# Two of the four parts of a causal convolution, first half: diagonal matmuls on TensorE in place of VectorE and ScalarE/GpSimd

## The chip, the cores and the metric

One NeuronCore of a Trainium2 chip runs the whole kernel. The metric is the device time of one execution in microseconds (us); lower is better. The kernel before has a median of 1479.4 us over three runs (1476.76 to 1481.39).

## What is computed

One layer of a sequence model on 1024 tokens of width 1024. What matters here, cut from the reference:

```python
p = h @ w_in                                   # 1024 -> 2*512 (conv) + RWKV inputs
u, u_gate = jnp.split(p_conv, 2, axis=-1)
u = u * jax.nn.sigmoid(u_gate)                 # 512 channels
u = causal_dwconv(u, conv_dw_w, conv_dw_b)     # 31 taps per channel, padded by 30 at the front
u = jax.nn.silu((layer_norm(u, LN_EPS) * conv_ln_g + conv_ln_b))
...                                            # RWKV branch: a recurrence over tokens gives y
m = jnp.concatenate([u, y], axis=-1) @ w_out   # token mix
x = x + gt_m * rms_norm(m, mix_post_g)
...                                            # feed-forward: w_up, 3-tap conv, silu gate, w_down
```

The depthwise convolution has 512 channels, so four parts of 128 channels (one channel per partition), and 31 taps. Everything is float32.

## The kernel before, in words

**Tiling.** Activations are kept transposed, channels on partitions and tokens on the free axis. The 1024 tokens are done in two halves of 512; the RWKV recurrence goes in four quarters of 256 tokens (`unit` prepares a quarter, with `prep`, `inverse` and `merge`; `chain` runs the recurrence over it; `finish` normalises it). Projections use float32 split in two float32r numbers: `weight` (L135 to L142) loads a 256 KB slab with SyncE (L138), rounds it on ScalarE (L140) and subtracts on GpSimd (L142). `project` then issues three matmuls per block of 128 inputs, high by high, high by low, low by high (L158 to L160). A projected tile of 128 outputs is two slabs, so 24 matmuls of 128x512. It goes into a PSUM bank of tag "m", of which there are two. Slabs have three buffers.

**The stage around the change.** After the first half's projections are done, the program writes, in this order: `filler[0] = conv(0, accs, 8)`; `lora` and `group_out`, the second half's projections for the RWKV branch (13 tiles, each drained by `shifted`); unit 2; `gate_in` and `glu`, the second half's other projections (10 tiles, and the gate's own matmuls at L491 to L494). `shifted` (L346) and `glu` (L364) end with `next(filler[0], None)`, so each finished tile lets the convolution issue a further piece. Unit 1 and the chains of quarters 0 and 1 stand before this in the program under a raised priority, and run at the same time. After it come `conv_norm` (layer norm and silu of the convolution), `split_in` into the high and low operands, then `out_proj_q` and `channel_in_q` for quarters 0 and 1, and the up-projection `up` of the feed-forward, which fills TensorE for most of the rest.

**Who orders the work.** A planner in the compiler places each instruction on its engine by priority and by its own estimate of when operands are ready; the order on an engine is then fixed. `tc.keep_in_program_order(i)` pins single taps to their place on the engine; in `conv` these are the first tap of every eight and ScalarE's operations.

**The convolution** is `conv` (L375). `load` (L380 to L387) makes the padded input of one part, 30 + 512 columns, in a slot of tag "cu" (one buffer, parts 0 to 2) or "cu3" (part 3): GpSimd clears 30 columns (L382), SyncE loads the rest (L385). `vector` does parts 0, 1 and 2 on VectorE, 31 operations each: the first at L393, then a multiply-add per tap at L396, accumulated in a PSUM bank of tag "v", the last one written to `cacc0` to `cacc2`. `scalar` does part 3: ScalarE multiplies by a tap (L400 for the first, L403 after it, into two slots of tag "ctmp") and GpSimd adds (L404). `taps` is 8: each call of the filler issues eight steps. The second half's convolution is the same generator with `taps` 3, called from `up`.

**What waits for it.** `conv_norm` (L420 to L443) needs all four parts. The operands that `split_in` writes (`hh_o`, `hl_o`, L453 and L454) lie in the slots that held the second half's normalised input, so they wait for the last of `glu`'s matmuls on them too. `out_proj_q(0)` (tile `o`) needs these and the first quarter from `finish`; `out_proj_q(1)` needs the second quarter, which `mix_in_q` loads (tile `q_mi`, L824) after `finish(1)`, and that follows the chain of quarter 1.

**Other names that the change touches.** The tiles `v` of the RWKV branch (tag "v" of pool `rw`, five buffers) are allocated in `v_tiles` (first half) and `group_back` (second half, loaded at L541). The slots of tag "ctmp" have 512 columns and also serve `ada_rest`, `conv_norm` and the tiles `m` of the out projection.

Of the kernel before, what the change touches and what calls it, by code (L numbers as in the profile page):

```python
# [7 lines left out]
F32 = mybir.dt.float32  # L8
F32R = mybir.dt.float32r
AF = mybir.ActivationFunctionType  # L10
ALU = mybir.AluOpType
# [3 lines left out]
P = 128  # L15
D = 1024
T = 1024
HT = 512
NK = D // P
QT = HT // 2  # L20
# [5 lines left out]
KC = 31  # L26
# [41 lines left out]
def build(nc, tc, I, O):  # L68
    V, S, G, TE = nc.vector, nc.scalar, nc.gpsimd, nc.tensor
# [7 lines left out]
    def slot(pool, tag, name, n=HT, bufs=1, dt=F32):  # L77
        return pool.tile([P, n], dt, name=f"{tag}_{name}", tag=tag, bufs=bufs)
# [14 lines left out]
    def col(name, j=0, n=1):  # L93
        o = _cols[name] + j
        return pv[:, o:o + n]
# [24 lines left out]
    th = mod[:, 0:8]  # L120
# [11 lines left out]
    def bank(name, tag="s", bufs={"m": 2, "s": 1, "w": 2, "c": 1, "y": 1, "v": 1}):  # L132
        return ps_pool.tile([P, 512], F32, name=name, tag=tag, bufs=bufs[tag])
# [11 lines left out]
    spare, rate = iter(()), 1  # L145
# [180 lines left out]
    cv = tc.alloc_tile_pool(name="cv", bufs=1, side="right")  # L326
    rw = tc.alloc_tile_pool(name="rw", bufs=1, reuse_waits="tile")
# [47 lines left out]
    def conv(half, accs, taps):  # L375

        cw = lambda ct, k: col("conv_w", ct * KC + k)

        def load(ct):
            u = slot(cv, "cu3" if ct == 3 else "cu", f"{half}_{ct}", 30 + HT)  # L380
            if half == 0:
                G.memset(u[:, 0:30], 0.0)  # L382
            else:
                nc.sync.dma_start(u[:, 0:30], ud[0][ct][:, HT - 30:])
            nc.sync.dma_start(u[:, 30:], ud[half][ct])  # L385
            accs[ct] = slot(cv, f"cacc{ct}", f"{half}_{ct}")
            return u  # L387

        def vector():

            for ct in range(3):
                u, acc = load(ct), bank(f"cv{half}_{ct}", "v")
                yield V.tensor_scalar(acc, u[:, 0:HT], cw(ct, 0), col("conv_b", ct), ALU.mult, ALU.add)  # L393
                for k in range(1, KC):
                    o = accs[ct] if k == KC - 1 else acc
                    yield V.scalar_tensor_tensor(o, u[:, k:k + HT], cw(ct, k), acc, ALU.mult, ALU.add)  # L396

        def scalar():
            u, acc = load(3), accs[3]
            yield S.activation(acc, u[:, 0:HT], AF.Identity, scale=cw(3, 0), bias=col("conv_b", 3))  # L400
            for k in range(1, KC):
                t = slot(cv, "ctmp", f"{half}_{k}", bufs=2)
                i = S.activation(t, u[:, k:k + HT], AF.Identity, scale=cw(3, k), bias=ZERO)  # L403
                G.tensor_tensor(acc, acc, t, ALU.add)  # L404
                yield i

        v, s = vector(), scalar()
        n = 0
        while n < 3 * KC:
            for j in range(taps):  # L410
                i = next(v, None)
                if i is not None and j == 0:
                    tc.keep_in_program_order(i)
                if n % 3 == 0:
                    i = next(s, None)
                    if i is not None:
                        tc.keep_in_program_order(i)
                n += 1
            yield

    def conv_norm(accs, half, b):
        s = slot(cv, "cu", f"s{half}", 30 + HT)[:, :HT]
        V.tensor_tensor(s, accs[0], accs[1], ALU.add)
        V.tensor_tensor(s, s, accs[2], ALU.add)
        V.tensor_tensor(s, s, accs[3], ALU.add)
        mean = bank(f"cm{half}", b)
        TE.matmul(mean, nmean, s, start=True, stop=True)
        s2 = slot(cv, "cu3", f"s2{half}", 30 + HT)[:, :HT]
        for ct in range(4):
            V.tensor_tensor(accs[ct], accs[ct], mean, ALU.add)  # L430
            sq = s2 if ct == 0 else slot(cv, "ctmp", f"sq{half}_{ct}", bufs=2)
            S.activation(sq, accs[ct], AF.Square, bias=ZERO)
            if ct:
                G.tensor_tensor(s2, s2, sq, ALU.add)
        rb = bcast(rstd(s2, f"cv{half}", ones, 1, 1.0 / CW, EPS_LN, tag="c", b=b), f"cv{half}", 1, b=b)
        for ct in range(4):
            V.tensor_tensor(accs[ct], accs[ct], rb, ALU.mult)
            t = slot(cv, "ctmp", f"th{half}_{ct}", bufs=2)
            S.activation(t, accs[ct], AF.Tanh, scale=col("ln_g", ct), bias=col("ln_b", ct))
            S.activation(accs[ct], accs[ct], AF.Identity, scale=col("ln_g", ct), bias=col("ln_b", ct))  # L440
            V.scalar_tensor_tensor(accs[ct], t, 1.0, accs[ct], ALU.add, ALU.mult)
            if half:
                nc.sync.dma_start(mixed[half][ct], accs[ct])  # L443
# [7 lines left out]
    def split_in(x, hh, hl):  # L451

        S.copy(hh, x)  # L453
        V.tensor_tensor(hl, x, hh.bitcast(F32), ALU.subtract)  # L454
        return hh, hl
# [50 lines left out]

    def v_tiles(half):

        new = lambda q, g: rw.tile([P, 2, QT], F32, name=f"v{2 * half + q}{g}", tag="v", bufs=5)
        t = {(q, g): new(q, g) for q, g in ((0, 0), (0, 1), (1, 0), (1, 1))}  # L510
        return [[t[q, g] for q in range(2)] for g in range(2)]

# [24 lines left out]
    def group_back(q, g):  # L537
        kvr = []
        for x in range(3):
            t = rw.tile([P, 2, QT], F32, name=f"{'kvr'[x]}{q}{g}", tag="kvr"[x], bufs=(3, 5, 3)[x])  # L540
            nc.sync.dma_start(t, kvd[g][x][:, q % 2])  # L541
            kvr.append({q % 2: t})
        return kvr
# [274 lines left out]
    mtags = ("ctmp", "ctmp", "cu", "cu3", "cacc0", "cacc1", "cacc2", "cacc3")  # L818
# [205 lines left out]
    def unit(q, kvrs, la, before=None):  # L1024
# [4 lines left out]
        if before:  # L1029
            with first():  # L1030
# [6 lines left out]
    kvrs = [in_group(h, 0, 0, vt[0])]  # L1037

    ctags = ("ctmp", "cu", "ctmp", "cu3", "cacc0")
    spare = ada_rest(range(3), lambda i, n: slot(cv, ctags[i % 5], n, 30 + HT if ctags[i % 5][:2] == "cu" else HT,  # L1040
                                                 2 if ctags[i % 5] == "ctmp" else 1)[:, :HT],
                     4, lambda n: slot(cv, "cacc2", n), "v")
    kvrs.append(in_group(h, 0, 1, vt[1]))
# [26 lines left out]
    accs = [None] * 4  # L1070
# [18 lines left out]
    with first():  # L1089
        for k in range(4):  # L1090
            split_in(accs[k], *h[k])
    ms = [slot(cv, t, f"m{m}", 30 + HT if t[:2] == "cu" else HT, 2 if t == "ctmp" else 1)[:, :HT] for m, t in enumerate(mtags)]
    with tc.high_priority(offset=500000):
        mix_in_q(0, h)
        sums = out_proj_q(0, h, ms)
# [11 lines left out]
    accs = [None] * 4  # L1107
# [29 lines left out]
def layout(inp):  # L1137

    a = {k: np.asarray(v) for k, v in inp.items()}
    c = np.ascontiguousarray  # L1140
    vec = lambda v: v.reshape(-1, P).T
    mu = a["rwkv_mu"][0]
    mu = np.concatenate([vec(mu[:1664 + 128]), np.pad(np.tile(mu[1792:], 3), (0, 32)).reshape(P, 1)], 1)
    taps = lambda w: w.reshape(w.shape[0], -1, P).transpose(2, 1, 0).reshape(P, -1)
    pv = np.concatenate([
        vec(a["c"][0]), vec(a["ada_b"][0]), vec(a["mix_pre_g"][0]), vec(a["mix_post_g"][0]),
        vec(a["ffn_pre_g"][0]), vec(a["ffn_post_g"][0]), taps(a["conv_dw_w"][0]),
        vec(a["conv_dw_b"][0]), vec(a["conv_ln_g"][0]), vec(a["conv_ln_b"][0]), mu,
        vec(a["w0"][0]), vec(a["a0"][0]), vec(a["k_k"][0]), vec(a["k_a"][0]),
        vec(a["r_k"][0].reshape(-1)), vec(a["lnx_g"][0]), vec(a["lnx_b"][0]),  # L1150
        taps(a["ffn_dw_w"][0]), vec(a["ffn_dw_b"][0])], 1)

    mt = lambda w: w.reshape(w.shape[0] // P, P, -1, P).transpose(2, 1, 0, 3).reshape(-1, P, w.shape[0])
    w_in = a["w_in"][0]
    cols = []
    for t in range(4):
        cols += [t, 4 + t]
    cols += [20, 21]
    for p in range(4):
        cols += [12 + p, 16 + p, 8 + p]  # L1160
    win = mt(w_in[:, :22 * P])[cols]
    winl = w_in[:, 22 * P:].reshape(8, P, 1, 32).transpose(1, 0, 2, 3).repeat(3, 2).reshape(P, 768)
    ada = a["ada_w"][0]
    am = ada.reshape(8, P, 6, 2, HT).transpose(2, 3, 0, 1, 4)
    ada1, ada2 = am[:2], am[2:]
    return {
        "pv": c(pv), "cst": constants(),
        "w2a2": c(np.concatenate([a["w2"][0], a["a2"][0]], 0)),
        "g2a": c(a["g2"][0][:128]), "g2b": np.tile(a["g2"][0][128:], (3, 1)),
        "xT": c(a["x"][0].T.reshape(8, P, 2, HT).transpose(2, 0, 1, 3)),  # L1170
        "xR": c(a["x"][0][HT:].reshape(4, P, 2, HT)), "ada1": c(ada1), "ada2": c(ada2), "w_in": c(win), "w_inl": c(winl),
        "w_out": c(mt(a["w_out"][0])), "w_up": c(mt(a["w_up"][0])),
        "w_down": c(mt(a["w_down"][0])),
    }
# [15 lines left out]
```

## Time and profile before

| what | value |
|---|---|
| median of three runs | 1479.4 us |
| the profiled execution's own time | 1478.22 us |
| its span in the trace | 1476.4 us |
| mean granted TensorE clock | 0.964 |
| TensorE matmul / weight load busy | 93% / 76% |
| VectorE, ScalarE, GpSimd busy | 62%, 46%, 53% |

Busy time is the union of an engine's instructions as the trace has them. A matmul of 128x512 lasts 0.39 us in the trace but the next one starts 0.23 us later, because matmuls overlap; a row of TensorE's busy time therefore says when it had something in flight, and the weight loads (PEld), which do not overlap each other, say better how much more would fit. The span is cut into stretches below: 206 to 467 us is the stretch of the second half's projections, 467 to 584 us that of the out projection of the first half, and from 584 us on TensorE runs the feed-forward.

### The profile page before, as it was taken

What the parts mean: (1) busy time and instruction counts of PE and PEld (TensorE: products, weight loads), DVE (VectorE), ACT (ScalarE), POOL (GpSimd) and SP (SyncE); (2) the same over time, 40 slices, a digit from 0 to 9 for tenths busy, and PEclk for the clock granted to TensorE, in tenths of its full rate; (3) what the DMA queues carried; (4) which work ended last, traced back from release to release, by engine and by line L of the source; (5) the groups of instructions that cost most, each with busy time, mean ns of one, the idle gap of its engine ahead of it and who ended that gap; (6) DMA issues with size and microseconds to landing.
All of it is one profiled execution on the core that took longest, in us unless ns stands there. A gap on an engine that the chain in (4) does not pass through costs nothing.

```text
span 1476.4 us, 23402 instructions
## 1 busy us (share of the span) xinstructions
PE 1379.4 (93%) x8412; PEld 1115.5 (76%) x8412; DVE 915.0 (62%) x1427; ACT 682.0 (46%) x1234; POOL 783.0 (53%) x716
## 2 busy tenths in 40 slices
PE   3999989999899997999999999999998999999995
PEld 2787867777577885777788787777887888888884
DVE  7667669899765466888779965562027555551102
ACT  5445354365553465444555454644233444443221
POOL 2545654588653354555666654457446555454443
PEclk9999989999899896999999999999999999999997
DMA  9394572345323753235337345883335323233332
GB/s 358 118 351 139 171 202 93 116 121 152 97 79 106 184 161 106 66 90 150 96 107 217 122 147 188 295 285 91 94 96 183 110 94 99 95 98 93 92 98 75
DMA packets 168484, 208.02 MB, mean 141 GB/s; under 512 B 64112, under 2 KB 79088, under 8 KB 168368
## 3 DMA queue, kind: packets, MB, share of 16 engines
q1 hardware_dynamic: 167792, 205.48, 44.5%
q8 instruction: 66, 1.08, 0.3%
q10 hardware_dynamic: 576, 1.05, 0.2%
q14 instruction: 50, 0.41, 0.1%
HBM read 172.39 MB, written 34.08 MB: 140 GB/s over the span
## 4 chain that ended last, share of the span: by engine, by line
PE 67%; DVE 18%; DMA 6%; issue 3%; ACT 2%; SPq 2%; POOL 1%; DVEq 0%; POOLq 0%; ACTq 0%
PE up L158 9%; PE up L159 9%; PE up L160 9%; PE d L160 5%; PE d L158 5%; PE d L159 5%; DVE cv L396 2%; PE o L160 1%; PE o L158 1%; PE o L159 1%; DVE rkp L599 1%; DVE bk L601 1%; DVE t_dx L678 1%; PE s L621 1%; PE hn L708 1%
## 5 line engine op out<-in xcount | busy, mean ns | idle before, releaser
L142 POOL TENSOR_TENSOR wl_up<-w_up,wh_up 128x512 fp32r<-128x512 f32 x176 | 236.6, 1346 | 190.3 <-ACT wh_up L140 173.3
L140 ACT CAST wh_up<-w_up 128x512 fp32r<-128x512 f32 x176 | 108.9, 619 | 198.2 <-PE up L159 121.3
L142 POOL TENSOR_TENSOR wl_dn<-w_dn,wh_dn 128x512 fp32r<-128x512 f32 x96 | 116.8, 1220 | 118.6 <-ACT wh_dn L140 117.0
L158 PE MATMUL up<-hh_o,wh_up 128*128 128x512 f32 x352 | 141.3, 402 | 4.3 <-DVE q_za L949 4.2
L158 PE MATMUL up<-hh_f,wh_up 128*128 128x512 f32 x352 | 138.0, 392 | 4.1 <-DVE q_za L949 4.1
L160 PE MATMUL up<-hh_o,wl_up 128*128 128x512 f32 x352 | 141.7, 403 | 0.0
L159 PE MATMUL up<-hl_o,wh_up 128*128 128x512 f32 x352 | 140.7, 400 | 0.0
L160 PE MATMUL d<-ah,wl_dn 128*128 128x512 f32 x352 | 139.4, 397 | 1.0 <-POOL wl_dn L142 1.0
L159 PE MATMUL d<-al,wh_dn 128*128 128x512 f32 x352 | 139.4, 396 | 0.0
L158 PE MATMUL d<-ah,wh_dn 128*128 128x512 f32 x352 | 139.3, 396 | 0.0
L160 PE MATMUL up<-hh_f,wl_up 128*128 128x512 f32 x352 | 137.5, 391 | 0.0
L159 PE MATMUL up<-hl_f,wh_up 128*128 128x512 f32 x352 | 137.4, 390 | 0.0
L396 DVE SCALAR_TENSOR_TENSOR cv<-cu,pv,cv 128x512 f32<-128x512 f32 x174 | 130.2, 748 | 2.3
L994 DVE TENSOR_SCALAR mo_f<-d,mod 128x512 f32<-128x512 f32 x16 | 12.0, 749 | 180.9 <-ACT q_sqd L993 169.6
L140 ACT CAST wh_dn<-w_dn 128x512 fp32r<-128x512 f32 x96 | 56.0, 584 | 146.6 <-PE d L159 121.5
L944 DVE SCALAR_TENSOR_TENSOR q_za<-up,pv,q_za 128x510 f32<-128x510 f32 x88 | 65.6, 745 | 88.4 <-ACT q_za L942 88.2
L404 POOL TENSOR_TENSOR cacc<-cacc,ctmp 128x512 f32<-128x512 f32 x60 | 79.0, 1316 | 48.8 <-ACT ctmp L403 38.5
L158 PEld LDWEIGHTS up<-hh_o,wh_up 128*128 128x128 f32 x352 | 67.4, 192 | 19.3 <-DVE q_za L949 4.8
L158 PEld LDWEIGHTS up<-hh_f,wh_up 128*128 128x128 f32 x352 | 66.5, 189 | 18.6 <-ACT wh_up L140 4.5
L160 PEld LDWEIGHTS d<-ah,wl_dn 128*128 128x128 f32 x352 | 66.1, 188 | 17.6 <-POOL wl_dn L142 1.9
L160 PEld LDWEIGHTS up<-hh_o,wl_up 128*128 128x128 f32 x352 | 67.4, 191 | 14.9 <-issue 0.5
L158 PEld LDWEIGHTS d<-ah,wh_dn 128*128 128x128 f32 x352 | 66.1, 188 | 16.2 <-ACT wh_dn L140 0.4
(449 smaller groups left out, 3466.8 us busy)
## 6 DMA issues: line engine op xcount, KB each, us to landing
w_up<-w_up SPq DMA_DIRECT2D x176, 256.0 KB, 2.6
w_dn<-w_down SPq DMA_DIRECT2D x80, 256.0 KB, 2.7
w_o<-w_out SPq DMA_DIRECT2D x48, 256.0 KB, 3.4
aw_ada<-ada SPq DMA_DIRECT2D x32, 256.0 KB, 5.4
act<-q_za SPq DMA_DIRECT2D x22, 256.0 KB, 2.1
ax<-act SPq DMA_DIRECT2D x22, 256.0 KB, 4.6
ctmp_adb<-ada SPq DMA_DIRECT2D x20, 256.0 KB, 4.9
cu_adb<-ada SPq DMA_DIRECT2D x19, 256.0 KB, 4.5
```

What stands on the lines that cost most here:

```text
L140: S.copy(hi, w)
L142: e.tensor_tensor(lo, w, hi.bitcast(F32), ALU.subtract)
L158: TE.matmul(ps, wh[:, o], xh, start=k == 0, stop=False)
L159: TE.matmul(ps, wh[:, o], xl, start=False, stop=False)
L160: TE.matmul(ps, wl[:, o], xh, start=False, stop=k == K - 1)
L396: yield V.scalar_tensor_tensor(o, u[:, k:k + HT], cw(ct, k), acc, ALU.mult, ALU.add)
L404: G.tensor_tensor(acc, acc, t, ALU.add)
L599: V.tensor_tensor(pic(rkp[x][:, :, 1 + hh, :])[r], part(kkn, x)[r], half(eprev, x)[r], ALU.mult)
L601: V.tensor_tensor(bk[r, :, 1 - hh, :], v3(k)[r], v3(einv)[r], ALU.mult)
L621: TE.matmul(pss[hh][:, d], bk[r, ci(x, d)], rkp[x][r, d, 0:2 + hh:1 + hh, :], start=True, stop=True)
L678: V.tensor_tensor(t[:, i], u.unsqueeze(2).broadcast_to([P, n, n, n]), v.rearrange("p s c -> p c s").unsqueeze(1).broadcast_to([P, n, n, n] ...
L944: V.scalar_tensor_tensor(a[:, 2:], ps[:, 0:HT - 2], fw(0), a[:, 2:], ALU.mult, ALU.add)
```

## The change

Parts 0 and 1 of the first half stay on VectorE. Parts 2 and 3 become matmuls: for each tap a diagonal 128x128 matrix with the tap's weights (made on the host, a new input `cdiag` of 4 x 128 x 3968 float32) times the shifted input. As in the projections, weights and input are split into high and low, three matmuls per tap. Part 3 is issued whole at the fourth call of the filler, part 2 whole at the ninth. The second half's convolution is not changed.

```diff
+        def tensor(cts):
+            for ct in cts:
+                u, ps = load(ct), bank(f"cd{half}_{ct}", "m")
+                uh = slot(cv, "ctmp", f"uh{half}_{ct}", 30 + HT, 2, F32R)
+                ul = slot(cv, "ctmp", f"ul{half}_{ct}", 30 + HT, 2, F32R)
+                S.copy(uh, u)
+                G.tensor_tensor(ul, u, uh.bitcast(F32), ALU.subtract)
+                for k0 in range(0, KC, 4):
+                    kn = min(4, KC - k0)
+                    wh, wl = weight(I["cdiag"][ct][:, k0 * P:(k0 + kn) * P], f"cd{half}_{ct}_{k0}", kn * P)
+                    for k in range(k0, k0 + kn):
+                        o, t = slice((k - k0) * P, (k - k0 + 1) * P), slice(k, k + HT)
+                        TE.matmul(ps, wh[:, o], uh[:, t], start=k == 0, stop=False)
+                        TE.matmul(ps, wh[:, o], ul[:, t], start=False, stop=False)
+                        TE.matmul(ps, wl[:, o], uh[:, t], start=False, stop=k == KC - 1)
+                    if k0 + kn == KC:
+                        S.activation(accs[ct], ps, AF.Identity, scale=0.5, bias=col("conv_b", ct))
+                    yield
-        def vector():
-            for ct in range(3):
+        def vector(cts):
+            for ct in cts:
...
-                t = slot(cv, "ctmp", f"{half}_{k}", bufs=2)
+                t = slot(cv, "ctmp", f"{half}_{k}", 30 + HT, 2)[:, :HT]
...
-        v, s = vector(), scalar()
+        if half == 0:
+            v = vector(range(2))
+            for n in range(100):
+                for j in range(taps):
+                    i = next(v, None)
+                    if i is not None and j == 0:
+                        tc.keep_in_program_order(i)
+                if n in (3, 8):
+                    for _ in tensor([c for c in range(2, 4) if (c == 3) == (n == 3)]):
+                        pass
+                if n > 8 and i is None:
+                    return
+                yield
+
+        v, s = vector(range(3)), scalar()
...
-        new = lambda q, g: rw.tile([P, 2, QT], F32, name=f"v{2 * half + q}{g}", tag="v", bufs=5)
+        new = lambda q, g: rw.tile([P, 2, QT], F32, name=f"v{2 * half + q}{g}", tag="v", bufs=4)
...
-            t = rw.tile([P, 2, QT], F32, name=f"{'kvr'[x]}{q}{g}", tag="kvr"[x], bufs=(3, 5, 3)[x])
+            t = rw.tile([P, 2, QT], F32, name=f"{'kvr'[x]}{q}{g}", tag="kvr"[x], bufs=(3, 4, 3)[x])
```

In `layout`, on the host, `cdiag` is built from the 31 taps. The slots of tag "ctmp" grow from 512 to 542 columns wherever they are used.

## Rows read from the trace of the kernel before

**Rows 1.** The page's busy times: engine, us, share, instructions.
```profile
PE 1379.4 (93%) x8412; PEld 1115.5 (76%) x8412; DVE 915.0 (62%) x1427; ACT 682.0 (46%) x1234; POOL 783.0 (53%) x716
```

**Rows 2.** Busy by stretch: length; PE, PEld, DVE, ACT, POOL; clock, DMA share, GB/s.
```profile
234.00:380.00 146.00, 138.19 (x1127) 108.27 (x1125) 135.12 (x221) 78.65 (x136) 101.72 (x97) 0.96 0.43 125
206.00:467.00 261.00, 245.14 (x2104) 188.75 (x2104) 208.12 (x351) 134.90 (x244) 163.88 (x149) 0.94 0.36 107
467.00:520.00 53.00, 49.14 (x427) 45.47 (x425) 27.98 (x49) 25.61 (x53) 18.45 (x17) 0.90 0.68 180
1000.00:1100.00 100.00, 99.60 (x437) 80.46 (x436) 16.54 (x24) 37.23 (x63) 56.51 (x48) 1.00 0.33 94
```

**Rows 3.** Instructions on `cu`, 225 to 380: ns min/median/max, first and last start.
```profile
L396 DVE SCALAR_TENSOR_TENSOR cv<-cu,pv,cv x87: 732/755/762, 235.8 to 371.9; 128x512 f32<-128x512 f32 x87
L403 ACT ACTIVATE ctmp<-cu,small,pv x30: 799/814/819, 296.1 to 376.1; 128x512 f32<-128x512 f32 x30
L393 DVE TENSOR_SCALAR cv<-cu,pv x3: 802/807/814, 234.5 to 326.9; 128x512 f32<-128x512 f32 x3
L396 DVE SCALAR_TENSOR_TENSOR cacc<-cu,pv,cv x3: 730/732/737, 275.4 to 374.3; 128x512 f32<-128x512 f32 x3
L385 SPq DMA_DIRECT2D cu<-u x2: 327/334/342, 276.2 to 320.0; - x2
```

**Rows 4.** Groups on GpSimd and ScalarE, 230 to 380: count, busy us, mean.
```profile
L404 POOL TENSOR_TENSOR cacc<-cacc,ctmp 128x512 f32<-128x512 f32 x30 | 40.1, 1336 | 7.8 <-ACT ctmp L403 7.0
L142 POOL TENSOR_TENSOR wl_r<-w_r,wh_r 128x512 fp32r<-128x512 f32 x8 | 10.8, 1346 | 5.8 <-ACT wh_r L140 5.8
L140 ACT CAST wh_r<-w_r 128x512 fp32r<-128x512 f32 x8 | 4.9, 618 | 6.8 <-issue 3.8 <-PE p_k L159 2.1 <-POOL zv L742 0.9
```

**Rows 5.** Chain of waits by line, 328 to 376, then 295 to 316.
```profile
by line: DVE cv L396 18.6%; SPq L696 10.6%; DMA w_u<-w_in 8.9%; DMA t_gtl<-gt 7.4%; SPq L688 7.1%; issue 6.0%; DVE ys L799 5.9%; DVE t_dx L678 4.9%; DVE ys L800 4.8%; DVE at L709 3.9%; DVE q_e L460 3.0%; DVE einv_cs L569 2.7%; DVE pc L577 2
...
by line: POOL cacc L404 25.5%; DVE cv L396 17.6%; issue 15.7%; POOL bk L630 9.0%; POOL zv L742 5.7%; POOL wl_v L142 4.8%; POOL wl_k L142 4.5%; ACT ctmp L403 4.0%; ACT q_s L354 3.7%; ACT wh_r L140 2.9%; DVE t_bv L611 2.8%; ACT bkt L635 1.7%;
```

**Rows 6.** Matmuls of a dense stretch in order of time: start us, duration us.
```profile
1009.61 0.40 PE L158 MATMUL d<-ah,wh_dn 128*128 128x512 f32 x1
...
1012.88 0.40 PE L160 MATMUL d<-ah,wl_dn 128*128 128x512 f32 x1
```

**Rows 7.** SyncE's waits 230 to 480 (us, times, longest); slab load's landing.
```profile
SPq L138 <- POOL q_s L353: 20.1, 8, 5.2
...
w_r<-w_in SPq DMA_DIRECT2D x15, 256.0 KB, 2.9
```

**Rows 8.** Readers of first-half `v`, and the loads of the second half's `v`.
```profile
L721 PE MATMUL vb<-cst,v x32: 218/218/267, 232.0 to 243.2; 64*64 64x64 f32 x32
...
L541 SPq DMA_DIRECT2D v<-vd x4: 319/326/425, 274.3 to 391.7; - x4
```

**Rows 9.** Hand-over to the out projection: tiles, TensorE's timeline, its groups 467 to 520.
```profile
L453 ACT CAST hh_o<-cacc x4: 606/618/623, 457.2 to 464.5; 128x512 fp32r<-128x512 f32 x4
...
467.37 0.40 PE L160 MATMUL p_u<-hh,wl_u 128*128 128x512 f32 x1
...
513.52 0.28 PE L160 MATMUL o<-hh_o,wl_o 128*128 128x256 f32 x1
...
L453 ACT CAST hh_o<-q_mi x4: 404/406/406, 516.9 to 520.5; 128x256 fp32r<-128x256 f32 x4
...
L701 PE MATMUL pt<-dd,at 64*64 64x64 f32 x64 | 3.6, 227 | 0.0
```

**Rows 10.** GpSimd's and VectorE's timelines around 321: start, duration us.
```profile
321.08 1.30 POOL L404 TENSOR_TENSOR cacc<-cacc,ctmp 128x512 f32<-128x512 f32 x1
...
321.14 1.27 DVE L665 TENSOR_TENSOR dm<-dm,t_dt 128x12 f32<-128x12 f32 x1
...
325.26 0.17 DVE L665 TENSOR_TENSOR dm<-dm,t_dt 128x12 f32<-128x12 f32 x1
```

More of the change, by code (lines that the diff above doesn't have):

```diff
@@ L430, in conv_norm @@
             V.tensor_tensor(accs[ct], accs[ct], mean, ALU.add)
-            sq = s2 if ct == 0 else slot(cv, "ctmp", f"sq{half}_{ct}", bufs=2)
+            sq = s2 if ct == 0 else slot(cv, "ctmp", f"sq{half}_{ct}", 30 + HT, 2)[:, :HT]
             S.activation(sq, accs[ct], AF.Square, bias=ZERO)
@@ L437, in conv_norm @@
             V.tensor_tensor(accs[ct], accs[ct], rb, ALU.mult)
-            t = slot(cv, "ctmp", f"th{half}_{ct}", bufs=2)
+            t = slot(cv, "ctmp", f"th{half}_{ct}", 30 + HT, 2)[:, :HT]
             S.activation(t, accs[ct], AF.Tanh, scale=col("ln_g", ct), bias=col("ln_b", ct))
@@ L1039, in build @@
     ctags = ("ctmp", "cu", "ctmp", "cu3", "cacc0")
-    spare = ada_rest(range(3), lambda i, n: slot(cv, ctags[i % 5], n, 30 + HT if ctags[i % 5][:2] == "cu" else HT,
+    spare = ada_rest(range(3), lambda i, n: slot(cv, ctags[i % 5], n, HT if ctags[i % 5] == "cacc0" else 30 + HT,
                                                  2 if ctags[i % 5] == "ctmp" else 1)[:, :HT],
@@ L1091, in build @@
             split_in(accs[k], *h[k])
-    ms = [slot(cv, t, f"m{m}", 30 + HT if t[:2] == "cu" else HT, 2 if t == "ctmp" else 1)[:, :HT] for m, t in enumerate(mtags)]
+    ms = [slot(cv, t, f"m{m}", HT if t[:4] == "cacc" else 30 + HT, 2 if t == "ctmp" else 1)[:, :HT] for m, t in enumerate(mtags)]
     with tc.high_priority(offset=500000):
@@ L1162, in layout @@
     winl = w_in[:, 22 * P:].reshape(8, P, 1, 32).transpose(1, 0, 2, 3).repeat(3, 2).reshape(P, 768)
+    cw = a["conv_dw_w"][0].reshape(KC, 4, P)
+    cdiag = np.zeros((4, P, KC, P), np.float32)
+    cdiag[:, np.arange(P), :, np.arange(P)] = cw.transpose(2, 1, 0)
+    cdiag = cdiag.reshape(4, P, KC * P)
     ada = a["ada_w"][0]
@@ L1170, in layout @@
         "xT": c(a["x"][0].T.reshape(8, P, 2, HT).transpose(2, 0, 1, 3)),
-        "xR": c(a["x"][0][HT:].reshape(4, P, 2, HT)), "ada1": c(ada1), "ada2": c(ada2), "w_in": c(win), "w_inl": c(winl),
+        "cdiag": cdiag, "xR": c(a["x"][0][HT:].reshape(4, P, 2, HT)), "ada1": c(ada1), "ada2": c(ada2), "w_in": c(win), "w_inl": c(winl),
         "w_out": c(mt(a["w_out"][0])), "w_up": c(mt(a["w_up"][0])),
```

## The prediction

> **What bounds the kernel now.** I read the page's busy times first: TensorE is busy for 93% of the span, VectorE for 62% [rows 1]. These are averages over stages, so I then cut the busy times by stretch. The change works in the stretch of the second half's projections, 206 to 467 us. Its part from 234 to 380 is the one to look at: VectorE is busy for 135.1 of 146 us, TensorE for 138.2 [rows 2]. Neither has much room.
>
> The convolution fills this part: its three VectorE parts begin at 234.5 and end at 374.3, and ScalarE's part runs beside the third from 296.1 to 376.1 [rows 3]. 87 taps at 0.755 us, three firsts at 0.807 and three lasts at 0.732 make 70.3 us, half of VectorE's busy time there. GpSimd adds 30 times at 1.336 us, 40.1 us [rows 4].
>
> The chain of waits shows what of it sets the pace. From 328 to 376, while part 2 is computed, 18.6% of the chain are taps; from 295 to 316, 25.5% are GpSimd's adds and 4.0% ScalarE's multiplications [rows 5]. So the convolution delays the second unit's preparation, which runs among it.
>
> Last I looked at the hand-over. The out projection's operands are written from 457.2 to 464.5, and the last projection matmul starts at 467.37 [rows 9]. The convolution is ready some 80 us before, so its own end is not late: it matters only through the engines it occupies.
>
> **The change, part by part.**
>
> *VectorE loses part 2.* 30 taps at 0.755 and a first at 0.807 are 23.5 us of work [rows 3]. On the path is what the chain shows: 18.6% of 48 us, 8.9 us [rows 5]. I take 8.9, between nothing (another wait takes the place) and 23.5.
>
> *ScalarE and GpSimd lose part 3's taps.* On the path: 25.5% + 4.0% of 21 us, 6.2 us [rows 5]. Against it stands the new work: each part has eight slabs of weights, so 16 roundings at 0.618 us and 16 subtractions at 1.346 [rows 4], and one rounding and one subtraction of the input, priced like a slab's, plus one drain of the bank, priced like L403 at 0.814 [rows 3]. ScalarE: 16 x 0.618 + 2 x 0.618 + 2 x 0.814 = 12.8 us for 31 x 0.814 = 25.2. GpSimd: 18 x 1.346 = 24.2 for 40.1. Both are relieved, so 6.2 stands. Its ends are 0 and the 12.4 us that ScalarE saves. Gain so far: 15.1 us.
>
> *TensorE gains 2 x 31 x 3 = 186 matmuls of 128x512.* In a dense stretch 14 of them take 1012.88 - 1009.61 = 3.27 us, 0.234 each [rows 6], so 43.4 us. How much room is there? By matmul busy time 261 - 245.1 = 15.9 us from 206 to 467. By the weight loads more: a full stretch has 80.46 us of them in 100, this one 188.75, which would fit in 234.6 us, leaving 26.4 [rows 2]. I take 26.4, since matmuls overlap in the busy time. Then 17.0 us do not fit (27.5 by the other count) and push the last projections later. Behind 467 there are 53 - 49.1 = 3.9 us of TensorE idle before 520 [rows 2], and 3.6 us of unit 2's merge (L701) [rows 9], at lower priority than the out projection, which can go later. That leaves 17.0 - 7.5 = 9.5 us on the path. Ends: 0 and 27.5.
>
> *Loads.* 16 slabs, 4.06 MB, go through SyncE's queue among the projections' slabs, which land in 2.9 us at the median. The longest wait of that queue before a slab is 5.2 us [rows 7]. Two further slabs are buffered, each worth 12 matmuls or 2.8 us, so 5.6 us cover it: cost 0; without the cover, at most the 5.2 us once or twice. The inputs' loads and their clears (L385, L382) are as many as before.
>
> *Bank, buffers, slots.* A block of 93 matmuls holds one of the two "m" banks for 21.7 us. The tile behind it has the other bank, and only the one after that needs the drain, 0.814 us twice: hidden by a tile's 24 matmuls, 5.6 us. If that cover fails it is 1.6 us. Tag "v" with four buffers costs 0: the buffer that the second half's first load takes is last read at 243.2, and that load is issued at 274.3 [rows 8]. Wider "ctmp" slots cost 0, as nothing more is computed in them.
>
> *Where the waits go.* "cu" has one buffer, so part 2 cannot start before part 1's last tap; its load is now issued at 320.0 [rows 3]. With a slab's landing of 2.9, rounding and subtraction 2.0, matmuls 21.7 and the drain 0.8, it would end at about 347 in place of 374. So VectorE and GpSimd are free earlier, the layer norm moves forward, and what is late next is TensorE: the last projection, and the chain of quarter 1 that lets the second quarter in (`q_mi`, rounded from 516.9 [rows 9]). The new blocks stand in TensorE's queue ahead of the later projection tiles, and behind these wait their ScalarE and VectorE drains; unit 1 and the chains have priority over both.
>
> **The sum.** -15.1 + 9.5 = -5.6 us. The profiled execution took 1478.2 us, 1.2 under the median of 1479.4; 1472.6 for it, or 1473.8 against the median.
>
> *A further gain, from GpSimd's adds.* At 321.14 a VectorE operation on 12 columns took 1.27 us, as long as the GpSimd add that began 0.06 us before; the same operation took 0.17 us at 325.26 [rows 10]. So such adds can stop VectorE for their whole length. GpSimd has 40.1 - 24.2 = 15.9 us less of them, and VectorE does other work than taps for 135.1 - 70.3 = 64.8 of 146 us, 44%: at most 7.0 us, which I leave to the range, because the added subtractions may do the same. The Trainium skill ("SBUF — State Buffer", section "SBUF: two separate sides") says that a GpSimd operation and a VectorE operation with two SBUF inputs take one shared port pair as an exclusive lock, for a whole instruction. These two durations agree; by that rule the sum would be -12.6 us instead of -5.6.
>
> **The rivals.**
>
> *TensorE becomes the bound: slower.* The projections' end frees the out projection's operands, so what VectorE gains is not on the path if TensorE is full. For it: 138.2 of 146 us busy, 43.4 us of new work and 26.4 of room. Against it: unit 1, which waited for VectorE and GpSimd, shapes TensorE's order too. Price: +9.5 with none of the 15.1, 1488.9; up to +17, 1496, if nothing is absorbed behind 467. It decides once the last projection comes more than 7.5 us after 467.4.
>
> *Nothing that counts moves.* The out projection's second quarter starts at 516.9 because of the chain of quarter 1, a sequence of small dependent matmuls; the last matmul of the first quarter starts at 513.5 [rows 9], so 3.4 us of delay is free there. If that chain keeps its pace, part 2 merely goes elsewhere. The change also does less than it says if part 2's block comes late because of the single "cu" buffer: then only the 6.2 us count, against 9.5. Price: 1479 within 4.
>
> *A larger gain.* The added matmuls fit, the 15.1 come out whole and some of the 7.0 with them: 1479.4 - 15.1 = 1464.3, down to 1457.3. For it: two engines are relieved in the very part where both are on the chain. Against it: TensorE would have to be filled more densely than from 234 to 380 now.
>
> **Chances.** About 0.3% (4.4 us) is what a measurement of this kernel can tell from no change. Forecast 0.36, larger gain 0.14, both faster: 0.50. Nothing moves 0.18. TensorE bound 0.32, slower. With both signs likely, the forecast's own range is 1468 to 1475. The whole range goes from 1458, nearly all of the larger gain, to 1494, most of the rival with TensorE bound.
>
> **What would show it.** Right: no GpSimd adds and 62 VectorE operations of the convolution in the first half, VectorE's share from 290 to 380 well under the 93% it has from 234 to 380, 186 more matmuls at a pitch near 0.234 us, weight loads above 72% of the projections' stretch, `q_mi` before 517 and the feed-forward's start earlier by some 6 us. Wrong: the last projection matmul after 475 with `q_mi` waiting behind it; TensorE idle ahead of a block for its slabs; or `q_mi` at 517 again with the convolution done by 350.

## The result, and the profile after

The changed kernel takes 1512.15 us (median of three, 1511.0 to 1516.2) against 1479.4. The ratio on record, from all runs of both, is 1.0235, 95% interval 1.0206 to 1.0265: slower by 34.8 us (the two medians differ by 32.75; what follows goes by the ratio). The profiled execution took 1516.2 us, its span 1514.4, 38.0 us over the span before.

Busy times of the page, to be held against [rows 1]:

```profile
PE 1417.9 (94%) x8598; PEld 1153.0 (76%) x8598; DVE 881.5 (58%) x1396; ACT 672.8 (44%) x1223; POOL 763.3 (50%) x704
```

The change did what it says: 186 matmuls more, VectorE 33.5 us less busy, GpSimd 19.7, ScalarE 9.2. Its cost is not in these sums. The same stretches as in [rows 2], then finer ones (length; PE, PEld, DVE, ACT, POOL; clock, DMA share, GB/s):

```profile
234.00:380.00 146.00, 131.51 (x1230) 105.01 (x1229) 92.76 (x168) 46.84 (x92) 58.05 (x59) 0.93 0.34 98
206.00:467.00 261.00, 245.48 (x2179) 193.85 (x2178) 155.07 (x281) 111.95 (x211) 124.79 (x123) 0.96 0.36 106
290.00:340.00 50.00, 40.02 (x307) 32.60 (x304) 38.10 (x72) 14.46 (x25) 21.13 (x24) 0.86 0.45 117
340.00:380.00 40.00, 35.72 (x468) 28.86 (x469) 10.49 (x21) 11.20 (x25) 9.38 (x8) 0.91 0.31 93
380.00:467.00 87.00, 86.95 (x587) 67.25 (x587) 43.76 (x85) 47.64 (x87) 47.23 (x47) 1.00 0.40 124
321.50:345.00 23.50, 11.76 (x131) 10.61 (x129) 12.94 (x22) 5.25 (x9) 5.03 (x7) 0.71 0.57 132
```

VectorE falls from 135.1 to 92.8 us between 234 and 380, as meant. TensorE, which got the work, is *less* busy there, 131.5 us for 138.2, and from 321.5 to 345 it stands half idle. From 380 to 467 it has no gap at all: 86.95 of 87 us.

To see what stood still, count one of the three matmuls of a projection (L160, eight per tile) by stretch. Before 450 us no other matmul has this line. The count behind the first busy time is the one to read. Kernel before:

```profile
206.00:290.00 84.00, 28.64 (x71) 13.91 (x71) 0.97 0.37 110
290.00:340.00 50.00, 18.05 (x46) 8.35 (x45) 1.00 0.41 119
340.00:380.00 40.00, 8.04 (x20) 3.79 (x20) 0.86 0.50 131
380.00:450.00 70.00, 15.96 (x36) 7.39 (x36) 0.89 0.29 94
```

Kernel after:

```profile
206.00:290.00 84.00, 14.18 (x36) 6.78 (x36) 0.99 0.29 87
290.00:340.00 50.00, 13.51 (x34) 6.38 (x34) 0.86 0.45 117
340.00:380.00 40.00, 0.00 (x0) 0.00 (x0) 0.91 0.31 93
380.00:450.00 70.00, 25.25 (x64) 11.82 (x64) 1.00 0.35 107
```

Up to 290 the count falls by 35, or 105 matmuls: about as many as part 3's 93, which took the projections' place. From 290 to 380 it falls by 32, and in the last 40 us not one projection matmul runs. After 380 a full TensorE catches up 28. Left at 450: 173 - 134 = 39, times 3 x 0.234 [rows 6] 27.4 us of projections late.

The instructions on the input of part 1 and part 2 (columns as in [rows 3]):

```profile
L416 DVE SCALAR_TENSOR_TENSOR cacc<-cu,pv,cv x2: 748/748/748, 269.9 to 332.0; 128x512 f32<-128x512 f32 x2
L385 SPq DMA_DIRECT2D cu<-u x2: 327/443/559, 270.7 to 339.1; - x2
L395 ACT CAST ctmp_uh<-cu x1: 644/644/644, 344.1 to 344.1; 128x542 fp32r<-128x542 f32 x1
```

Part 1's last tap starts at 332.0 (it was 319.3 before, though part 1 then began later). Only then is the single "cu" buffer free; part 2's load is issued at 339.1, behind SyncE's transfers of `dm` and `dd`, which it issues from 328.5 on, and its input is rounded at 344.1. The first entry of part 2's block in TensorE's timeline (start, us, and in brackets the idle time before it and its releaser):

```profile
344.80 0.51 PE L402 MATMUL cd<-ctmp_uh,wh_cd 128*128 128x512 f32 x1 [1.77 <-ACT ctmp_uh L395]
```

and the last of each tap's three diagonal matmuls, from 290 on:

```profile
L404 PE MATMUL cd<-ctmp_uh,wl_cd x31: 388/397/628, 351.4 to 383.4; 128*128 128x512 f32 x31
```

So the block waits until 344.8 and then takes until 383.4, 38.6 us for 21.7 of matmuls, and the merge and the chain of the quarter run among it. The remaining tiles of `group_out` stand behind it on TensorE, and their slabs behind its slabs on SyncE. SyncE's waits from 230 to 480 (us, times, longest), against 28.9 for the projections' drains:

```profile
SPq L138 <- POOL wl_cd L142: 38.6, 10, 8.7
SPq L138 <- POOL q_s L353: 28.9, 9, 5.6
```

The hand-over, against [rows 9]: last projection, the second quarter's rounding, and the feed-forward's first matmul, the latter for the kernel before too (first and last start until 660 us):

```profile
L158 PE MATMUL up<-hh_o,wh_up x62: 387/391/774, 584.7 to 659.8; 128*128 128x512 f32 x62
```

```profile
L160 PE MATMUL p_u<-hh,wl_u x10: 388/389/397, 480.0 to 495.8; 128*128 128x512 f32 x10
L488 ACT CAST hh_o<-q_mi x4: 400/401/405, 544.9 to 546.4; 128x256 fp32r<-128x256 f32 x4
L158 PE MATMUL up<-hh_o,wh_up x37: 387/393/774, 615.7 to 658.4; 128*128 128x512 f32 x37
```

The last projection starts 28.4 us late (495.8 for 467.4), the second quarter 28.0, the feed-forward 31.0. The remaining 7.0 us come in the feed-forward. The granted clock over its first 100 us is 0.91 for 0.95 before; but it is 0.91 with part 3 alone on TensorE too (below), where the feed-forward takes as long as before (892.2 us for 891.7). No run went after these 7 us, and the profiled execution is the slowest of the three (spans 1514.4, 1507.9, 1510.2).

### The profile page after: what moved, and what is told of

The parts are those of the page before. It is cut to its first block, busy times and chain, and to the rows that moved or that the text cites. A ratio compares the mean times of both kernels' runs of the same rounds, so it can differ in the third digit from the quotient of the medians.

```text
span 1514.4 us, 23777 instructions
## 1 busy us (share of the span) xinstructions
PE 1417.9 (94%) x8598; PEld 1153.0 (76%) x8598; DVE 881.5 (58%) x1396; ACT 672.8 (44%) x1223; POOL 763.3 (50%) x704
## 4 chain that ended last, share of the span: by engine, by line
PE 71%; DVE 15%; DMA 8%; issue 2%; POOL 1%; ACT 1%; SPq 1%; DVEq 0%; POOLq 0%; ACTq 0%
PE up L159 9%; PE up L158 9%; PE up L160 9%; PE d L160 5%; PE d L158 5%; PE d L159 5%; DVE cv L416 2%; PE o L160 2%; PE o L158 2%; PE o L159 2%; DVE rkp L634 1%; DMA t_gtl<-gt 1%; PE s L656 1%; DMA aw_ada<-ada 1%; DVE bk L636 1%
## 5 line engine op out<-in xcount | busy, mean ns | idle before, releaser
L160 PE MATMUL up<-hh_o,wl_up 128*128 128x512 f32 x352 | 142.7, 405 | 0.0
L160 PE MATMUL d<-ah,wl_dn 128*128 128x512 f32 x352 | 139.5, 397 | 1.3 <-POOL wl_dn L142 1.3
L160 PE MATMUL up<-hh_f,wl_up 128*128 128x512 f32 x352 | 137.8, 391 | 0.0
L416 DVE SCALAR_TENSOR_TENSOR cv<-cu,pv,cv 128x512 f32<-128x512 f32 x145 | 108.5, 748 | 1.6
L142 POOL TENSOR_TENSOR wl_o<-w_o,wh_o 128x512 fp32r<-128x512 f32 x32 | 45.3, 1420 | 74.4 <-ACT wh_o L140 68.2
L160 PEld LDWEIGHTS d<-ah,wl_dn 128*128 128x128 f32 x352 | 66.1, 188 | 18.2 <-POOL wl_dn L142 2.6
L160 PEld LDWEIGHTS up<-hh_o,wl_up 128*128 128x128 f32 x352 | 67.8, 193 | 15.2 <-issue 0.5
```

The costliest lines, as they stand in the source:

```text
L142: e.tensor_tensor(lo, w, hi.bitcast(F32), ALU.subtract)
L160: TE.matmul(ps, wl[:, o], xh, start=False, stop=k == K - 1)
```

## The experiments

Microseconds below are (ratio - 1) x 1479.4, so that runs beside different medians can be compared. The planner orders every one of these kernels anew, so two runs can differ by more than the edit that is shown.

**The relief alone.** Parts 2 and 3 of the first half become one ScalarE operation each; 30 taps of each part are left out, and there are no slabs or diagonal matmuls.

```diff
-                u, ps = load(ct), bank(f"cd{half}_{ct}", "m")
...
+                u = load(ct)
+                S.activation(accs[ct], u[:, 0:HT], AF.Identity, scale=cw(ct, 0), bias=col("conv_b", ct))
+                yield
```

> The changed kernel without the diagonal matmuls and their weights: parts 2 and 3 get one tap only, by a single ScalarE operation each, so 30 taps of each are left out and nothing is put in their place. It measures what the relief of VectorE, ScalarE and GpSimd is worth by itself. Theory T (TensorE bounds the stretch of the projections, so what the other engines do there counts little): 1473 us, 0 to 8 less than before. Rival V (the waits for VectorE and GpSimd were on the path, as the forecast had it): 15 us less or better, 1461.

Ratio 0.9916 (0.9895 to 0.9938): -12.4 us. The last projection matmul:

```profile
L160 PE MATMUL p_u<-hh,wl_u x8: 389/389/397, 446.6 to 456.0; 128*128 128x512 f32 x8
```

The last one starts 11.4 us earlier than before. The gain lies above theory T's 8 us, and rival V's 15 is within its interval: the relieved engines did set the pace, by about what I had said.

**The matmuls alone.** The kernel before, its convolution untouched, plus a block of 93 matmuls on resident operands at the fourth call of the filler, or that and a second one at the ninth (the edit shown is the second run's; the first has `(3,)`).

```diff
+            ps = bank(f"bare{n}", "m")
+            for k in range(93):
+                TE.matmul(ps, h[k % 8][0][:, 0:P], h[(k + 1) % 8][0], start=k == 0, stop=k == 92)
+            S.activation(cp.tile([P, 1], F32, name=f"bare{n}", tag="bare", bufs=1), ps[:, 0:1], AF.Identity, bias=ZERO)
...
+            if half == 0 and calls in (3, 8):
+                bare(calls)
```

> The kernel before, its convolution untouched, with 93 matmuls of 128x512 added at the fourth call of the filler, on operands that are there anyway; nothing is loaded, rounded or relieved, the result is not used. 21.7 us of TensorE work alone. Theory T: as much as part 3 on TensorE cost, about 14 us, 1490 (1486 to 1497). Rival V: they fit into the 26.4 us of room; at most 1481.

> The same with two such blocks, at the fourth and the ninth call: 43.4 us of TensorE work and no relief. Theory T: about what the change cost and a little more, 1511 us (1505 to 1518). Rival V: 17 us over the room, 1494 at most.

One block: 1.0049 (1.0033 to 1.0066), +7.2 us for 21.7 us of matmuls. Two: 1.0177 (1.0155 to 1.0199), +26.2 for 43.4. Both stand at the lower end of theory T's ranges, and over rival V's limits. By the whole time 14.5 us fit in the first run and 17.2 in the second. By the traces it is less even. The last projection comes 12.0 us late with one block (479.4 for 467.4) and 17.6 with two, so 9.7 and 25.8 us fit ahead of it. With two the feed-forward starts at 603.8, 19.1 us late, and the span is 26.2 longer (1502.6 for 1476.4), so 7.1 us more are lost in the feed-forward, as in the change. The last projection with both blocks:

```profile
L160 PE MATMUL p_u<-hh,wl_u x24: 388/389/477, 451.6 to 485.0; 128*128 128x512 f32 x24
```

L160 by stretch with both blocks:

```profile
206.00:290.00 84.00, 13.89 (x35) 6.87 (x35) 0.95 0.23 58
290.00:340.00 50.00, 14.24 (x36) 6.57 (x35) 1.00 0.43 114
340.00:380.00 40.00, 6.36 (x16) 3.12 (x17) 0.96 0.32 93
380.00:450.00 70.00, 22.13 (x56) 10.17 (x56) 1.00 0.41 127
```

The early loss of 36 is here too, without any wait; the empty stretch from 340 to 380 is not.

**The wait taken away.** Part 2's input gets the slot of part 3 in place of part 1's.

```diff
-            u = slot(cv, "cu3" if ct == 3 else "cu", f"{half}_{ct}", 30 + HT)
+            u = slot(cv, "cu3" if ct == 3 or (ct == 2 and half == 0) else "cu", f"{half}_{ct}", 30 + HT)
```

> Part 2's input goes into the slot of part 3 (tag cu3), which is free once part 3 is rounded, so its block no longer waits for part 1's last tap on VectorE. Theory W (the waiting block): in the changed kernel TensorE's projections stand still from 321.5 us, because part 2's block stands in its order ahead of them and waits for that tap until 344.6; that is some 20 of the 33 us. Then this run is at 1492 us (1487 to 1497) and the hole is gone. Rival C (capacity): the 43.4 us of added matmuls do not fit wherever they stand; then 1505 us or more.

1.0182 (1.0159 to 1.0205): +26.9, so 7.9 us less than the change. Busy by stretch, TensorE is full again from 290 to 340 (49.10 us for 40.02 in the change):

```profile
290.00:340.00 50.00, 49.10 (x358) 38.60 (x356) 38.97 (x74) 14.85 (x26) 25.00 (x26) 1.00 0.45 119
```

and of the L160 matmuls 12 come back from 340 to 380:

```profile
340.00:380.00 40.00, 5.01 (x12) 2.25 (x12) 0.96 0.43 127
```

The wait is real, and by these middle values it is under a quarter of the loss; theory W, which gave it some 20 us, does not hold.

**The block put later.** Part 2's block at the fourteenth call in place of the ninth.

```diff
-                if n in (3, 8):
+                if n in (3, 13):
...
-                if n > 8 and i is None:
+                if n > 13 and i is None:
```

> Part 2's block is issued at the fourteenth call of the filler in place of the ninth, behind the remaining tiles of group_out, which then need not wait for it. Theory W: as with its own slot, 1492 us (1486 to 1498), and no stretch from 320 to 345 without projections. Rival C: 1505 us or more, as the amount of work on TensorE is the same.

1.0239 (1.0212 to 1.0267): no different from the change, as rival C had it. The block no longer waits (its input is rounded at 349.3, its first matmul starts at 378.7), and nothing is gained: a wait can be taken away without its price coming back. The projections now keep on until 380, and fall back after it; the last comes at 516.2, yet the end is where the change has it. From there to the feed-forward's first matmul, at 623.0, it is 106.8 us in place of the change's 119.9; what shortens it was not found out.

**Slabs and order without most of the matmuls.** As the change, all 16 slabs and both blocks in place, but two matmuls per slab, 32 in all; the other products are left out. The first run keeps part 2's wait, the second takes it away with the slot of part 3, as above.

```diff
-                    for k in range(k0, k0 + kn):
...
+                    TE.matmul(ps, wh[:, 0:P], uh[:, k0:k0 + HT], start=k0 == 0, stop=False)
+                    TE.matmul(ps, wl[:, 0:P], uh[:, k0:k0 + HT], start=False, stop=k0 + kn == KC)
```

> The changed kernel with all 16 slabs loaded, rounded and subtracted, but two matmuls per slab in place of twelve: 32 of 186, so most taps are left out. Theory S: the relief's 11.3 us, less some 10 for the slabs, less 3 to 11 for the few matmuls and the block's wait: 1480 to 1488 us. Rival I: the slabs cost nothing, 1468 to 1474.

> As the run with all slabs and two matmuls per slab (32 in all, the other products of the two parts left out), and part 2's input has the slot of part 3, so that it need not wait for part 1's last tap. That run lay 20 us above the kernel before, 31 above the relief alone. If the wait is what holds the projections there, it goes here with the wait: 1472 to 1482. If the 16 slabs themselves hold them (SyncE's queue, the roundings, three buffers), or a block's fixed place ahead of the projections does, the wait is worth no more than its 8 us in the full change: 1487 to 1495.

With the wait 1.0137 (1.011 to 1.0164), +20.3, above both theories; without it 0.9997 (0.9977 to 1.0017), -0.4, where the first of the two guesses had it. They differ by 20.7 us. L160 by stretch, with the wait:

```profile
340.00:380.00 40.00, 2.54 (x6) 1.13 (x6) 0.82 0.37 109
```

and without:

```profile
340.00:380.00 40.00, 11.02 (x28) 5.17 (x28) 1.00 0.59 180
```

That these 20.7 us are the price of the wait is not shown. The run with one product per tap (below) has the same slabs and the same wait, 5.6 us of idle TensorE right ahead of part 2's block for 5.9 here, and more matmuls, yet it costs 9.9 us and keeps its projections from 340 on:

```profile
340.00:380.00 40.00, 10.57 (x26) 4.88 (x26) 0.91 0.52 157
```

What else holds them back with 32 matmuls, a new order for one, no run separates.

**No slabs.** As the change, with the weights of the diagonal matmuls taken from the resident input, so nothing is loaded, rounded or subtracted for them; the product is another one. The second run has part 2's own slot too.

```diff
-                    wh, wl = weight(I["cdiag"][ct][:, k0 * P:(k0 + kn) * P], f"cd{half}_{ct}_{k0}", kn * P)
...
-                        o, t = slice((k - k0) * P, (k - k0 + 1) * P), slice(k, k + HT)
+                        t, (wh, wl) = slice(k, k + HT), h[k % 8]
...
```

> The changed kernel with its 186 matmuls and their inputs as they are, but on weights that are in SBUF anyway (the first 128 columns of the normalised input) in place of the diagonal ones: the 16 slabs' loads, roundings and subtractions are left out, so the convolution's parts 2 and 3 come out as something else. The parts measured so far are 11.3 us gained by the relief, 27.5 lost by bare matmuls, some 8 lost by the waiting block; with the 34 of the change that leaves 10. Theory S (the slabs cost those 10): 1502 us (1498 to 1506). Rival I (once TensorE is full the relief of the other engines counts for nothing, slabs or not): 1511 us (1507 to 1515).

> Both: part 2's input in the slot of part 3, and no slabs. What is left is the relief and 186 matmuls that wait for nothing but their inputs. Theory S, parts adding up: 1477.8 - 11.3 + 27.5 = 1494 us (1490 to 1498). Rival I: 1503, as with its own slot and slabs.

1.0218 (1.02 to 1.0235), 2.5 us under the change; 1.0156 (1.0136 to 1.0175), 3.8 under the run with the slot alone. The intervals overlap in both pairs: by their middle values the slabs cost up to some 4 us, and perhaps nothing. Both runs lie nearer rival I than theory S. Against each other they price the wait a second time: 9.2 us, beside 7.9 with the slabs.

**Fewer matmuls.** One product per tap of the three (62 matmuls, the low parts left out), and part 3 alone on TensorE with part 2 back on VectorE.

```diff
-                        TE.matmul(ps, wh[:, o], ul[:, t], start=False, stop=False)
-                        TE.matmul(ps, wl[:, o], uh[:, t], start=False, stop=k == KC - 1)
...
```

```diff
-            v = vector(range(2))
+            v = vector(range(3))
...
-                if n in (3, 8):
+                if n == 3:
...
```

> Leaves out the two products with the low parts in the convolution's matmuls: 62 matmuls in place of 186, 29 us less work for TensorE; loads, roundings, subtractions and the waiting block stay. Rival C: the time falls by nearly all of the 29 us, to 1483 (1479 to 1488). Theory W: part 1's last tap on VectorE stays where it is, so the hole takes back what part 3's shorter block saves, and only the shorter block of part 2 counts, some 14 us: 1498 (1493 to 1503).

> Only part 3 runs on TensorE; part 2 stays on VectorE as before the change. 21.7 us of added matmuls, no block that waits for VectorE, ScalarE and GpSimd relieved. Theory W: between 1474 and 1487 us. Rival C: half of the loss, about 1496 us.

One product: 1.0067 (1.0041 to 1.0092), +9.9. Leaving out 124 matmuls, 29.0 us, takes 24.9 us off, near rival C. Part 3 alone: 1.0105 (1.0076 to 1.0135), +15.5, rival C's half of the loss. Half the change is slower as well, and by 8.3 us more than 93 bare matmuls (+7.2; the intervals do not meet), although ScalarE and GpSimd are relieved. What part 3 adds to its matmuls (slabs, input, another order) was not taken apart.

**The buffers alone.** The kernel before with four buffers for `v` and the wider "ctmp".

```diff
-tag="v", bufs=5)
+tag="v", bufs=4)
...
```

> The kernel before with only the buffers of the change: tag v with four buffers, ctmp slots of 542 columns. Both theories: the same as before, within 3 us. If it is more, part of the loss is the buffers'.

0.9999 (0.9974 to 1.0024): nothing, within some 4 us.

## Why the prediction was wrong

The runs put side by side:

| | no added matmuls | 186 added, no slabs, no wait |
|---|---|---|
| without the relief | 0 | +26.2 |
| with the relief | -12.4 | +23.1 |

To the last field come 3.8 us of slabs (with them and the slot: 26.9) and 7.9 of the wait (34.8, the change). These three runs are one chain, so that sum comes out by itself. (The 7.9 is the difference of two ratios with half-widths of 0.003 and 0.0023, each 4 us or so; the shares are good to a few us.)

*The step that failed: "The sum. -15.1 + 9.5".* The two summands are not independent. "VectorE loses part 2" and "ScalarE and GpSimd lose part 3's taps" came out by themselves: forecast 15.1, measured 12.4 (9.2 to 15.5). But with the matmuls there the relief is worth 26.2 - 23.1 = 3.1 us (by the two intervals 7.4 at most, and perhaps nothing), and the last projection comes no earlier for it (485.4, and 485.0 without the relief). The stretch from 206 us to the last projection, in this order: before; the relief alone; two bare blocks; both (the relief and 186 matmuls, no slabs, no wait); the change (columns as in [rows 2]).

```profile
206.00:467.40 261.40, 245.54 (x2106) 189.07 (x2106) 208.12 (x351) 134.90 (x244) 164.28 (x149) 0.94 0.36 107
206.00:456.00 250.00, 236.49 (x2158) 184.05 (x2157) 178.08 (x328) 112.27 (x213) 120.93 (x119) 0.98 0.39 112
206.00:485.00 279.00, 273.75 (x2332) 217.07 (x2332) 194.05 (x352) 134.59 (x242) 159.57 (x148) 0.98 0.35 98
206.00:485.40 279.40, 272.11 (x2344) 215.63 (x2344) 171.09 (x313) 113.97 (x214) 123.86 (x121) 0.99 0.34 100
206.00:495.80 289.80, 274.03 (x2326) 216.63 (x2325) 176.01 (x313) 121.71 (x227) 141.04 (x136) 0.96 0.37 109
```

Length times what the granted clock lacks to 1 estimates, to some 1.5 us, what a lowered clock can take at most: 15.7 us before, 5.0 with the relief, 5.6 with the bare blocks, 2.8 with both. So the relief's 11.4 us come with 10.7 less of low clock, and TensorE's idle time falls only from 15.9 to 13.5 us. The bare blocks come with 10.1 less of the same low clock, and with idle time down from 15.9 to 5.2. The reading that fits is that either takes what TensorE lost there, and that it can be taken once; no run holds idle time or clock fixed to prove it. The prediction had this as a rival ("what VectorE gains is not on the path if TensorE is full") and not in the sum.

*"TensorE gains 186 matmuls", 9.5 us on the path: 26.2 measured.* The 17.0 us by which I had the last projections late came out as 17.6 with both bare blocks. That is partly luck: by the same 26.4 us of room one block alone would have fitted whole, and it makes the last projection 12.0 late. Of one block 9.7 us fitted ahead of the last projection, of two 25.8, so neither count (26.4 by weight loads, 15.9 by matmul busy time) is a room that added work simply fills up. The Trainium skill ("Perfetto Trace Analysis", section "Identifying the Most-Contended Engine") says to judge TensorE's headroom by MFU (the share of its peak arithmetic) and the share of weight loads, and not by that of matmuls. The count by weight loads is near the 25.8 of both blocks and far from the 9.7 of one. What was wrong is what follows: 7.5 us were to be absorbed, and 1.5 came on top, then 7.1 in the feed-forward, a term that I did not have. That my other count, 27.5, is near 26.2 is luck too.

*"7.5 us absorbed behind 467": none.* From the last projection to the feed-forward's first matmul it was 584.7 - 467.4 = 117.3 us, and is 615.7 - 495.8 = 119.9 (118.8 with the bare blocks). Other runs do shorten it, to 106.8 with the block later, so some of it can be used; when, no run shows.

*"Where the waits go": named and not priced.* I wrote that part 2 cannot start before part 1's last tap and had its load issued at 320.0; the tap came at 332.0, the load at 339.1, the block's end at 383.4 and not at 347. I priced the matmuls that the block would take and not what stands behind a block that waits: the rest of `group_out` on TensorE and its slabs on SyncE. A slot of its own is worth 7.9 us here, and 9.2 without slabs. The rival "Nothing that counts moves" saw the late block, and priced it by the lost relief alone.

*"Loads: cost 0": off by up to 3.8 us.* The longest wait before a slab was also misread: [rows 7] has 5.2 us for one releaser, and the same view of the kernel before has a longer one (us, times, longest):

```profile
SPq L138 <- POOL wl_u L142: 14.5, 3, 10.2
```

So the change's 8.7 is not longer than what was there.

*"A further gain, from GpSimd's adds", up to 7.0 us:* not seen. The relief alone has all of part 3's adds gone, and its 12.4 us stay below the 15.1 that were counted without this.

*Held:* buffers and slots at 0 (0.9999; the bank has no run of its own); 186 matmuls; VectorE's share from 290 to 380, (38.10 + 10.49) / 90 = 54%; the sign that was to prove the forecast wrong, the last projection after 475 with `q_mi` behind it. Weight loads above 72% of the stretch held as well (193.85 / 261 = 74%), so that sign told nothing.

The rival with TensorE as the bound was right in kind, and its condition met. Its price, up to 1496, was too low: with the 26.2 us of the bare blocks it is 1505.6, and the wait and the slabs, less what the relief still gives, make the rest.

## What to carry to other kernels

When work moves to an engine that is already near full, don't add the gain on the relieved engines to the cost on the loaded one: both can draw on the same lost time of the loaded engine, its idle time and its lowered clock. Estimate or measure "relief alone" and "load alone", and expect less than their sum of gains. A block of instructions at a fixed place is not priced by its own length alone: ask what is queued behind it when its input is late. A room on TensorE that is counted from busy shares is not a figure to subtract from; a bare block of matmuls at the place in question shows what fits there.

## What was not expected of the hardware

A TensorE that had stood idle also came back slower. In the change it has no matmul in flight from 321.8 to 326.4 us, at a clock of 1.00 until 325; from 328 to 340 the granted clock is 0.50, the lower of its two levels (1.2 and 2.4 GHz), and from 340 to 346, with matmuls in flight from 335.5 on, 1.00 again (the row at 343 is not shown):

```profile
328.00:331.00 3.00, 2.13 (x10) 2.01 (x10) 2.69 (x5) 0.72 (x1) 0.50 (x2) 0.50 0.29 33
337.00:340.00 3.00, 3.00 (x38) 2.66 (x37) 0.69 (x1) 0.14 (x1) 0.00 (x0) 0.50 0.81 189
340.00:343.00 3.00, 3.00 (x70) 2.77 (x70) 1.48 (x3) 0.45 (x1) 0.00 (x0) 1.00 0.98 234
```

From 380 to 467, where it has no gap, the clock is 1.00. Over the whole stretch to the last projection the change has a higher clock than the kernel before, 0.96 for 0.94, so the clock there does not explain the loss; it is 0.99 with part 2's own slot. How much of the wait's price is clock and how much is waiting, no run separates.
